# One root per block in the norms, and three constants loaded at other times, in a hybrid decoder layer on one core

## The chip, the cores and the metric
The kernel runs on one core of a Trainium2 chip. The metric is the device time of one execution in microseconds (us). The core has five instruction queues that run side by side and wait for each other by semaphores: TensorE (PE, matmuls and transposes), VectorE (DVE), ScalarE (ACT), GpSimd (POOL) and SyncE (SP, which here only issues DMAs; SPq in the trace). P is 128, the number of partitions; D is 1024, the width of the model.

## The reference
One layer over 1024 tokens and 16 meta tokens in front of them, all in float32. Two RMS norms stand in it: one with the scale vector g_mix ahead of the mixer (latent attention and retention, gated and merged), one with g_ffn ahead of the expert mixer (PEER).

```python
def rmsnorm(x, g):
    y = x * lax.rsqrt(jnp.mean(x * x, axis=-1, keepdims=True) + EPS)
    return y * g

def mixer_sublayer(h, pos, g_mix, w_in, ...):
    hn = rmsnorm(h, g_mix)
    z = hn @ w_in                          # queries, keys, values, gates of both branches
    ...
    merged = sigmoid(za) * y_a + sigmoid(zr) * y_r
    return merged @ w_mix_out

def peer_sublayer(h, g_ffn, w_peer_q, ...):
    x = rmsnorm(h, g_ffn)
    q = x @ w_peer_q                       # then top 16 of 128x128 experts per head, gathered and summed
    ...

h = h + mixer_sublayer(...);  h = h[:, N_META:];  h = h + peer_sublayer(...)
```

## The kernel before
The 1024 tokens are eight blocks of 128. They go in three groups, of three, two and three blocks; the first group carries the meta tokens as a fourth tile. Each group runs through the same stages, and a group's first stage is interleaved with the last part of the group before it.

- **latents (L345 to L372).** The blocks' x tiles are loaded (tile xt, L357; the meta rows L355), then g_mix, broadcast over the partitions (L360). `norm_scale` (L253) gives one scale per row, L363 multiplies xt by it and by g_mix, and PE transposes the result in 128x128 pieces (L272), four to a PSUM tile "tr" of which there are two. ACT copies the tile to hn_hi, the high part in fp32r (L275), and DVE takes the rest as hn_lo (L276); only then is the PSUM tile free again. In group 0 each block is transposed right behind its scale, in the others all at the end.
- **mix and merge.** The branches, their gates and the merge, whose result is mT (L857, L858). Queries go out to DRAM and back (qT_d, L557).
- **output (L868 on).** x is loaded again into h2 (L884), w_mix is multiplied and added into it block by block (`residual`, L886). Then g_ffn is loaded (L904), `norm_scale` runs over the h2 blocks, L908 makes xnt (two buffers), xnt is transposed into xT_hi and xT_lo, and the w_pq matmuls use those. The pool of g_ffn and xnt opens where that of mT has been closed, so the space of g_ffn is that of tiles that the last w_mix matmuls still read.
- Behind the groups stands the dense part of the experts (from about 1425 us to the end); rows gathered by POOL and dotted by DVE (L1071, L1088) run beside groups 1 and 2 and beside the dense part.

`norm_scale` squares a row and sums it on ACT (`square_sum`, L251), makes v = mean + eps on DVE (L262) and takes v to the power -0.5 on POOL (`rsqrt`, L213). It does so for block 0 alone, and then for all other blocks together, with one v and one root as wide as their number.

A dense product is three fp32r matmuls (`mm3`, L245 to L247): whi with hn_hi, with hn_lo, and wlo with hn_hi. Weights come through three "raw" buffers (L234) and are split by ACT (whi, L217) and DVE (wlo, L218).

At the top level the x tiles, the meta rows and g_mix of group 0 are issued first (`next(first)` runs up to the first yield of latents), then the constants (ident, g_cols, masks, iota, the rotary scales, keys), then HEAD = 20 further steps of group 0's latents, and then everything else. Routing (top experts per head) has its own pool, fc, opened at the head of output(); its tile "oh" (128x2048 in bf16, the same bytes as 128x1024 in float32) is used only while experts are picked.

A framework puts each engine's instructions into a static order and adds the waits. SP issues its DMAs strictly in that order, and one that waits holds those behind it.

Of the kernel before, what the change touches and what calls it, by code (L numbers as in the profile page):

```python
# [12 lines left out]
F32 = mybir.dt.float32  # L13
BF16 = mybir.dt.bfloat16
# [4 lines left out]
OP = mybir.AluOpType  # L19
# [4 lines left out]
P = 128  # L24
D = 1024
# [9 lines left out]
EPS = 1e-6  # L35
H = 8
# [11 lines left out]
DELAY = 8.0  # L48
STEPS = (((86, 72), (116, 64), (116, 144)), ((112, 90), (112, 100), (112,)), (80, 50))
HEAD = 20  # L50
BUBBLE = 12
LEAVE = ((6, 6, 3), (0, 1, 1))
RATES = ((0.0, 0.0), (0.5, 0.2), (0.3, 0.3), (0.8, 0.2), (0.9, 0.45), (0.0, 0.52))
# [91 lines left out]
def hybrid_layer(ctx: ExitStack, tc: tile.TileContext, out, a, dbg=None):  # L145
    nc = tc.nc
    V, S, T, G = nc.vector, nc.scalar, nc.tensor, nc.gpsimd
    dbg = dbg or {}

    const = ctx.enter_context(tc.tile_pool(name="const", bufs=1))  # L150
    work = ctx.enter_context(tc.tile_pool(name="work", bufs=2))
# [42 lines left out]
    def bcast(ap, n, off=0):  # L194
        return bass.AP(tensor=ap.tensor, offset=ap.offset + off, ap=[[0, P], [1, n]])
# [15 lines left out]
    def rsqrt(v, n, name, bufs=2):  # L211
        y = work.tile([P, n], F32, name=name, bufs=bufs)
        G.tensor_tensor(y, v, mhalf[:, 0:n], OP.pow)  # L213
        return y
# [34 lines left out]
    def square_sum(src, acc):  # L249
        junk = mw.tile([P, TW], F32, name="zt").bitcast(BF16)  # L250
        S.activation(junk[:, :src.shape[-1]], src, AF.Square, accum_out=acc)  # L251

    def norm_scale(tiles, name):  # L253

        n = len(tiles)
        ss = work.tile([P, n], F32, name=f"ss_{name}")
        v = work.tile([P, n], F32, name=f"v_{name}")
        for k in (slice(0, 1), slice(1, n)):
            for i in range(n)[k]:
                square_sum(tiles[i], ss[:, i:i + 1])  # L260
            if range(n)[k]:
                V.tensor_scalar(v[:, k], ss[:, k], 1.0 / D, EPS, op0=OP.mult, op1=OP.add)  # L262
                r = rsqrt(v[:, k], len(range(n)[k]), f"r_{name}{k.start}")
                for i in range(n)[k]:
                    yield i, r[:, i - k.start:i - k.start + 1]

    def transposed(dst, src, i):

# [46 lines left out]
    def group(g):  # L315
# [4 lines left out]
        meta, last = g == 0, g == len(GROUPS) - 1  # L320
# [4 lines left out]
        def pool(name, side="left"):  # L325
            return open_pool(f"{name}{g}", side)
# [20 lines left out]
        def latents():  # L347
            hn = own.hn
            nps, npool = pool("np")
            xs = []  # L350
            for b in every:
# [4 lines left out]
                else:  # L356
                    nc.sync.dma_start(xt, a["x"][P * b:P * b + P])  # L357
                xs.append(xt)
            g_mix = npool.tile([P, D], F32, name="g_mix")
            nc.sync.dma_start(g_mix, bcast(a["g_mix"], D))  # L360
            yield
            for i, r in norm_scale(xs, "x"):
                V.scalar_tensor_tensor(xs[i], xs[i], r, g_mix, op0=OP.mult, op1=OP.mult)  # L363
                yield
                if not g:
                    transposed(hn, xs[i], i)
            if g:
                for _ in range(BUBBLE):
                    yield
# [481 lines left out]
        def output():  # L851
# [4 lines left out]
            for c in range(KD):  # L856
                S.activation(mT[0][:, c], own.mg[:, c], AF.Copy, scale=0.5)  # L857
                V.scalar_tensor_tensor(mT[1][:, c], own.mg[:, c], 0.5, mT[0][:, c].bitcast(F32),  # L858
                                       op0=OP.mult, op1=OP.subtract)
# [12 lines left out]
            if not last:  # L872
                if g >= NGROUP:
                    ktp = ctx.enter_context(tc.tile_pool(name=f"kt{g}", bufs=1, side="right", reuse_waits="tile"))
                fcs, fc = pool("fc", "right")
# [4 lines left out]
            xT = [xp.tile([P, KD, W], F32R, name=n) for n in ("xT_hi", "xT_lo")]  # L880
            hps, hp_ = pool("h2", "right")
            h2 = hp_.tile([P, nbk, D], F32, name="h2")
            for i, b in enumerate(blocks):
                nc.sync.dma_start(h2[:, i], a["x"][P * b:P * b + P])  # L884
            def residual(i, c, z):
# [14 lines left out]


            fps, fp = pool("fp", "right")
            g_ffn = fp.tile([P, D], F32, name="g_ffn")
            nc.sync.dma_start(g_ffn, bcast(a["g_ffn"], D))  # L904
            for i, r in norm_scale([h2[:, i] for i in range(nbk)], "f"):
                b = blocks[i]
                xn = fp.tile([P, D], F32, name="xnt", bufs=2)
                V.scalar_tensor_tensor(xn, h2[:, i], r, g_ffn, op0=OP.mult, op1=OP.mult)  # L908
                nc.sync.dma_start(h2_d[b], h2[:, i])
                if g < NGROUP:  # L910
                    nc.sync.dma_start(xn_d[b], xn)
                transposed(xT, xn, i)
# [35 lines left out]

        own.right = g % 2 == 1
        own.open_inputs, own.latents, own.open_mix, own.mix = open_inputs, latents, open_mix, mix  # L950
        own.open_merge, own.merge, own.output = open_merge, merge, output
        return own
# [326 lines left out]
    first = groups[0].latents()  # L1279
# [5 lines left out]
    g_gn, g_ql, g_kvl = g_cols[:, 0:8], g_cols[:, 8:11], g_cols[:, 11:13]  # L1285
    g_gnh = const.tile([P, 8], F32, name="g_gnh")
    V.tensor_scalar(g_gnh, g_gn, 0.5, None, op0=OP.mult)
    mask_a, mask_r = (mw.tile([P, P], F32, name=n, bufs=1) for n in ("mask_a", "mask_r"))
    nc.sync.dma_start(mask_a, a["c_mask_a"])
    mask_b, ident_b = (mw.tile([P, P], BF16, name=n, bufs=1) for n in ("mask_b", "ident_b"))  # L1290
# [12 lines left out]
                                                      ap=[[1, 64], [1, 1]]))  # L1303
    gk96 = const.tile([P, 1], F32, name="gk96")
    V.tensor_tensor(gk96, gqk[:, 0:1], gqk[:, 1:2], OP.mult)
    ones = const.tile([P, 1], F32, name="ones")
    V.memset(ones, 1.0)
    keys = const.tile([P, 256], F32, name="keys")
    V.memset(keys, 0.0)
    nc.sync.dma_start(keys[0:64, 0:128], a["keys"][0:64])  # L1310
    nc.sync.dma_start(keys[64:128, 128:256], a["keys"][64:128])

    for _ in range(HEAD):
        next(first)
    interleave([first, groups[0].retentions], STEPS[2], 0)
    for n, now in enumerate(groups):
# [28 lines left out]
```

## Time and profile before

| | |
|---|---|
| median of 3 runs | 3475.97 us (3467.64 to 3477.73) |
| the profiled execution | 3464.74 us, of it 3463.0 us span |
| PE busy | 3293.4 us, 95% |
| PE weight loads (overlap PE) | 3003.2 us, 87% |
| DVE busy | 2609.1 us, 75% |
| ACT busy | 1266.3 us, 37% |
| POOL busy | 1118.6 us, 32% |
| DMA | 835.80 MB, 241 GB/s over the span |

The span is the time from the first to the last instruction of one profiled execution; all times of the trace are counted from its start. A row of the timeline reads: start, duration, engine, line, operation, what is written and what is read, shapes, count, and in brackets the idle time of the engine just before and what ended it. A row of the chain of waits is start, duration and piece of work.

### The profile page before, as it was taken

The page shows a single profiled execution, that of the slowest core. Times are in us where ns is not written, and L with a number is a line of the kernel's source. Part 1 is how long each engine was busy: PE and PEld are TensorE (multiplying, and loading weights), DVE is VectorE, ACT ScalarE, POOL GpSimd, SP SyncE. Part 2 cuts the span into 40 slices and gives each one's busy share as a digit, 9 for nine tenths or more (in the row PEclk, how much of TensorE's full clock was granted, in tenths as well). Part 3 has the DMA queues.
Part 4 walks back from the last instruction along what each step waited for, and adds up shares of the span by engine and source line. Part 5 has one row for each costly group of instructions (what it writes and reads, how often), then busy time and mean ns, then how long its engine had stood idle before and what let it go on. Part 6 is the DMA issues. An engine that isn't in the chain of part 4 may idle for free.

```text
span 3463.0 us, 53189 instructions
## 1 busy us (share of the span) xinstructions
PE 3293.4 (95%) x20376; PEld 3003.2 (87%) x20376; DVE 2609.1 (75%) x5118; ACT 1266.3 (37%) x2117; POOL 1118.6 (32%) x821
## 2 busy tenths in 40 slices
PE   8899999989889999999999999999999999999999
PEld 7788988888777799999999987988898888888888
DVE  4434458987697566689999786888788878878885
ACT  3445344554445533324666322222222222222221
POOL 0100010113211122012322444555556545555562
PEclk9999999999899999999999999999999999999999
DMA  4322354457744458545878998999889898989895
GB/s 133 124 72 92 122 178 149 142 178 242 261 149 149 132 199 293 174 158 197 312 287 297 350 313 288 338 316 325 312 308 342 297 327 311 337 309 326 303 327 188
DMA packets 326673, 835.80 MB, mean 241 GB/s; under 512 B 45697, under 2 KB 138113, under 8 KB 323601
## 3 DMA queue, kind: packets, MB, share of 16 engines
q1 hardware_dynamic: 215824, 429.69, 36.0%
q0 software_dynamic: 110592, 402.70, 33.0%
q8 instruction: 160, 2.62, 0.3%
q14 instruction: 97, 0.79, 0.1%
HBM read 753.85 MB, written 78.43 MB: 240 GB/s over the span
## 4 chain that ended last, share of the span: by engine, by line
PE 35%; issue 23%; POOL 10%; DVE 9%; DMA 7%; ACT 2%; SPq 0%; POOLq 0%; DVEq 0%; ACTq 0%
POOL row L1071 10%; PE zacc L245 7%; PE zacc L246 6%; PE zacc L247 6%; PE tr L245 3%; PE tr L246 3%; PE tr L247 3%; DMA row<-in_peer_v_dram,eidx 3%; DVE wlo L218 2%; DMA gl<-gl_d 2%; PE tr L766 2%; PE sc L730 1%; DVE row L1088 1%; DMA row<-in_peer_u_dram,eidx 1%; PE sc L776 1%
## 5 line engine op out<-in xcount | busy, mean ns | idle before, releaser
L217 ACT ACTIVATE whi<-raw 128x1024 fp32r<-128x1024 f32 (+2 forms) x508 | 520.4, 1026 | 1333.5 <-PE zacc L247 610.0
L218 DVE TENSOR_TENSOR wlo<-raw,whi 128x1024 fp32r<-128x1024 f32 (+2 forms) x508 | 599.7, 1181 | 405.6 <-ACT whi L217 404.9
L1071 POOL DMA_INDIRECT row<-in_peer_u_dram,eidx x384 | 500.0, 1302 | 992.7 <-DVE row L1088 761.2
L1071 POOL DMA_INDIRECT row<-in_peer_v_dram,eidx x384 | 555.2, 1446 | 649.7 <-DVE acc L1097 279.6
L245 PE MATMUL zacc<-whi,c_hi 128*128 128x512 f32 x1280 | 505.0, 395 | 36.8 <-DVE y L1270 34.4
L247 PE MATMUL zacc<-whi,c_lo 128*128 128x512 f32 x1280 | 503.1, 393 | 5.3 <-DVE c_lo L218 5.3
L246 PE MATMUL zacc<-wlo,c_hi 128*128 128x512 f32 x1280 | 502.6, 393 | 0.0
L1088 DVE SCALAR_TENSOR_TENSOR row<-row,xn 128x1024 f32<-128x1024 f32 x384 | 462.0, 1220 | 32.3 <-DMA row<-in_peer_u_dram,eidx 24.1
L245 PE MATMUL tr<-xT_hi,whi 128*128 128x384 f32 (+1 forms) x1216 | 411.7, 339 | 4.9 <-ACT gl L1181 3.8
L247 PE MATMUL tr<-xT_hi,wlo 128*128 128x384 f32 (+1 forms) x1216 | 408.9, 336 | 0.0
L246 PE MATMUL tr<-xT_lo,whi 128*128 128x384 f32 (+1 forms) x1216 | 408.8, 336 | 0.0
L245 PEld LDWEIGHTS zacc<-whi,c_hi 128*128 128x128 f32 x1280 | 243.4, 190 | 92.0 <-issue 32.1
L245 PE MATMUL tr<-x_hi,whi 128*128 128x256 f32 x1024 | 293.7, 287 | 0.6 <-DVE xT_lo L276 0.6
L247 PEld LDWEIGHTS zacc<-whi,c_lo 128*128 128x128 f32 x1280 | 243.0, 190 | 58.8 <-DVE c_lo L218 7.4
L246 PE MATMUL tr<-x_lo,whi 128*128 128x256 f32 x1024 | 289.1, 282 | 0.0
L247 PE MATMUL tr<-x_hi,wlo 128*128 128x256 f32 x1024 | 288.7, 282 | 0.0
L246 PEld LDWEIGHTS zacc<-wlo,c_hi 128*128 128x128 f32 x1280 | 243.6, 190 | 49.9
L1097 DVE SCALAR_TENSOR_TENSOR acc<-row,dots,acc 128x1024 f32<-128x1024 f32 x192 | 245.7, 1280 | 16.0 <-DMA row<-in_peer_v_dram,eidx 15.8
L245 PE MATMUL zacc<-whi,hn_hi 128*128 128x256 f32 x832 | 251.3, 302 | 6.4 <-DVE vr L680 4.1
L1097 DVE SCALAR_TENSOR_TENSOR xn<-row,dots,xn 128x1024 f32<-128x1024 f32 x189 | 241.7, 1279 | 11.8 <-DMA row<-in_peer_v_dram,eidx 11.7
L246 PE MATMUL zacc<-wlo,hn_hi 128*128 128x256 f32 x832 | 239.5, 288 | 0.9 <-DVE wlo L218 0.9
L245 PEld LDWEIGHTS tr<-xT_hi,whi 128*128 128x128 f32 x1216 | 232.0, 191 | 6.7 <-ACT gl L1181 4.4
(269 smaller groups left out, 6933.9 us busy)
## 6 DMA issues: line engine op xcount, KB each, us to landing
raw<-in_peer_ut_dram SPq DMA_DIRECT2D x128, 512.0 KB, 5.1
raw<-in_peer_vt_dram SPq DMA_DIRECT2D x128, 512.0 KB, 6.5
gate_d<-stage SPq DMA_DIRECT2D x20, 2048.0 KB, 7.8
gt<-gate_d SPq DMA_DIRECT2D x31, 1280.0 KB, 10.6
raw<-in_w_nat_dram SPq DMA_DIRECT2D x72, 512.0 KB, 3.5
raw<-in_w_z_dram SPq DMA_DIRECT2D x48, 512.0 KB, 3.4
gl_d<-gl SPq DMA_DIRECT2D x48, 320.0 KB, 3.3
gl<-gl_d SPq DMA_DIRECT2D x48, 320.0 KB, 8.1
```

Of the source, the lines that this page charges most:

```text
L217: S.activation(hi, src, AF.Copy)
L218: V.tensor_tensor(lo, src, hi.bitcast(F32), OP.subtract)
L245: T.matmul(o, st[0], mv[0], start=first, stop=False)
L246: T.matmul(o, st[0], mv[1], start=False, stop=False)
L247: T.matmul(o, st[1], mv[0], start=False, stop=last)
L730: T.matmul(sc[:, c, 0:w], qh, kT[0:96, k0:k0 + w], start=True, stop=c < nch - 1)
L766: T.matmul(oo, vh[:, c + k], pT[:, k], start=False, stop=c + k == b)
L776: T.transpose(pt[:, P * k:P * k + P], pr[:, k0:k0 + P], ident)
L1071: G.indirect_dma_start(out=row, out_offset=None, in_=table, in_offset=bass.IndirectOffsetOnAxis(ap=eidx[:, k:k + 1], axis=0))
L1088: op = V.scalar_tensor_tensor(row, row, 1.0, xn, op0=OP.mult, op1=OP.mult, accum_out=dots[:, k:k + 1])
L1097: op = V.scalar_tensor_tensor(acc[k % 2], row, dots[:, k:k + 1], acc[k % 2], op0=OP.mult, op1=OP.add)
```

## The change
`norm_scale` takes a v and a root for every block by itself. g_mix is loaded behind the first x tile and ahead of the others. In groups 0 and 1 g_ffn goes into the routing pool's tile "oh", viewed as 128x1024 float32, and its load stands ahead of the h2 loads; the last group keeps its own tile. At the top level, eight of the 20 steps of group 0's latents come ahead of the masks, iota, the rotary scales and the keys, and `ones` is set earlier.

```diff
+EARLY = 8
     def norm_scale(tiles, name):
-        n = len(tiles)
-        ss = work.tile([P, n], F32, name=f"ss_{name}")
-        v = work.tile([P, n], F32, name=f"v_{name}")
-        for k in (slice(0, 1), slice(1, n)):
-            for i in range(n)[k]:
-                square_sum(tiles[i], ss[:, i:i + 1])
-            if range(n)[k]:
-                V.tensor_scalar(v[:, k], ss[:, k], 1.0 / D, EPS, op0=OP.mult, op1=OP.add)
-                r = rsqrt(v[:, k], len(range(n)[k]), f"r_{name}{k.start}")
-                for i in range(n)[k]:
-                    yield i, r[:, i - k.start:i - k.start + 1]
+        for i, t in enumerate(tiles):
+            ss = work.tile([P, 1], F32, name=f"ss_{name}")
+            square_sum(t, ss)
+            v = work.tile([P, 1], F32, name=f"v_{name}")
+            V.tensor_scalar(v, ss, 1.0 / D, EPS, op0=OP.mult, op1=OP.add)
+            yield i, rsqrt(v, 1, f"r_{name}")
...
                 xs.append(xt)
-            g_mix = npool.tile([P, D], F32, name="g_mix")
-            nc.sync.dma_start(g_mix, bcast(a["g_mix"], D))
+                if len(xs) == 1:
+                    g_mix = npool.tile([P, D], F32, name="g_mix")
+                    nc.sync.dma_start(g_mix, bcast(a["g_mix"], D))
...
             h2 = hp_.tile([P, nbk, D], F32, name="h2")
+            if not last:
+                g_ffn = fc.tile([P, 8, 16, 2 * H], BF16, name="oh").rearrange("p a b c -> p (a b c)").bitcast(F32)
+                nc.sync.dma_start(g_ffn, bcast(a["g_ffn"], D))
             for i, b in enumerate(blocks):
                 nc.sync.dma_start(h2[:, i], a["x"][P * b:P * b + P])
...
             fps, fp = pool("fp", "right")
-            g_ffn = fp.tile([P, D], F32, name="g_ffn")
-            nc.sync.dma_start(g_ffn, bcast(a["g_ffn"], D))
+            if last:
+                g_ffn = fp.tile([P, D], F32, name="g_ffn")
+                nc.sync.dma_start(g_ffn, bcast(a["g_ffn"], D))
...
     V.tensor_scalar(g_gnh, g_gn, 0.5, None, op0=OP.mult)
+    ones = const.tile([P, 1], F32, name="ones")
+    V.memset(ones, 1.0)
+    for _ in range(EARLY):
+        next(first)
     mask_a, mask_r = (mw.tile([P, P], F32, name=n, bufs=1) for n in ("mask_a", "mask_r"))
...
-    for _ in range(HEAD):
+    for _ in range(HEAD - EARLY):
         next(first)
```

The lines of the changed kernel are shifted by a few: v is L260 there, the scale L360, hn_lo and xT_lo L272, wlo L219, xnt L909.

DVE at the start of the program, first before, then after; v_x is the mean of squares, xt the scaled tile, hn_lo what frees a transpose buffer.

```order
L262 TENSOR_SCALAR v_x<-ss_x 128x1
L262 TENSOR_SCALAR v_x<-ss_x 128x3
L363 SCALAR_TENSOR_TENSOR xt<-xt,r_x_163,g_mix 128x1024
L1287 TENSOR_SCALAR g_gnh<-g_cols 128x8
L1292 CAST ident_b<-ident 128x128
L363 SCALAR_TENSOR_TENSOR xt<-xt,r_x_187,g_mix 128x1024
L1291 CAST mask_b<-mask_a 128x128
L1296 CAST iota_i<-iota 128x256
L363 SCALAR_TENSOR_TENSOR xt<-xt,r_x_187,g_mix 128x1024
L276 TENSOR_TENSOR hn_lo<-tr,hn_hi 128x4x128
L1305 TENSOR_TENSOR gk_150<-gqk 128x1
L276 TENSOR_TENSOR hn_lo<-tr,hn_hi 128x4x128
```

```order
L260 TENSOR_SCALAR v_x<-ss_x 128x1
L360 SCALAR_TENSOR_TENSOR xt<-xt,r_x,g_mix 128x1024
L260 TENSOR_SCALAR v_x<-ss_x 128x1
L360 SCALAR_TENSOR_TENSOR xt<-xt,r_x,g_mix 128x1024
L260 TENSOR_SCALAR v_x<-ss_x 128x1
L360 SCALAR_TENSOR_TENSOR xt<-xt,r_x,g_mix 128x1024
L1288 TENSOR_SCALAR g_gnh<-g_cols 128x8
L260 TENSOR_SCALAR v_x<-ss_x 128x1
L1297 CAST ident_b<-ident 128x128
L360 SCALAR_TENSOR_TENSOR xt<-xt,r_x,g_mix 128x1024
L272 TENSOR_TENSOR hn_lo<-tr,hn_hi 128x4x128
L219 TENSOR_TENSOR wlo<-raw,whi 128x1024
```

Each scale now has its own v ahead of it, all four scales stand ahead of the first hn_lo (before, three), and a wlo follows that hn_lo; before, a second hn_lo, the scale of tile 3 and two more hn_lo came ahead of the first wlo.

DVE at the end of group 0's output stage, from its third-last residual add on, before and after; v_f is the mean of squares of an h2 block, xT_lo the counterpart of hn_lo.

```order
L886 TENSOR_TENSOR h_4889<-zacc,h_4889 128x256
L262 TENSOR_SCALAR v_f<-ss_f 128x1
L886 TENSOR_TENSOR h_4889<-zacc,h_4889 128x256 x2
L218 TENSOR_TENSOR wlo<-raw,whi 128x1024 x2
L262 TENSOR_SCALAR v_f<-ss_f 128x2
L908 SCALAR_TENSOR_TENSOR xnt<-h_4889,r_f_5257,g_ffn 128x1024
L908 SCALAR_TENSOR_TENSOR xnt<-h_4889,r_f_5282,g_ffn 128x1024
L276 TENSOR_TENSOR xT_lo<-tr,xT_hi 128x4x128 x2
L908 SCALAR_TENSOR_TENSOR xnt<-h_4889,r_f_5282,g_ffn 128x1024
L276 TENSOR_TENSOR xT_lo<-tr,xT_hi 128x4x128 x4
```

```order
L260 TENSOR_SCALAR v_f<-ss_f 128x1
L886 TENSOR_TENSOR h_4903<-zacc,h_4903 128x256
L260 TENSOR_SCALAR v_f<-ss_f 128x1
L886 TENSOR_TENSOR h_4903<-zacc,h_4903 128x256
L909 SCALAR_TENSOR_TENSOR xnt<-h_4903,r_f,oh 128x1024 x2
L260 TENSOR_SCALAR v_f<-ss_f 128x1
L219 TENSOR_TENSOR wlo<-raw,whi 128x1024
L272 TENSOR_TENSOR xT_lo<-tr,xT_hi 128x4x128 x2
L219 TENSOR_TENSOR wlo<-raw,whi 128x1024
L272 TENSOR_TENSOR xT_lo<-tr,xT_hi 128x4x128 x2
L909 SCALAR_TENSOR_TENSOR xnt<-h_4903,r_f,oh 128x1024
L272 TENSOR_TENSOR xT_lo<-tr,xT_hi 128x4x128 x2
```

The two wlo moved from ahead of the first xnt to places between the xT_lo, and xnt reads "oh".

SP around the same loads in group 0, before and after; acc is a first copy of h_d, the stored h2.

```order
L884 DMA h_4889<-in_x_dram 128x1024 x3
L234 DMA raw<-in_w_mix_dram 128x1024 x4
L234 DMA raw<-in_w_pq_dram 128x1024 x4
L909 DMA h_d<-h_4889 128x1024 x2
L1080 DMA acc<-h_d 128x1024
L904 DMA g_ffn<-in_g_ffn_dram 128x1024
L909 DMA h_d<-h_4889 128x1024
```

```order
L884 DMA h_4903<-in_x_dram 128x1024 x2
L882 DMA oh<-in_g_ffn_dram 128x1024
L884 DMA h_4903<-in_x_dram 128x1024
L235 DMA raw<-in_w_mix_dram 128x1024 x4
L235 DMA raw<-in_w_pq_dram 128x1024 x4
L910 DMA h_d<-h_4903 128x1024 x2
```

g_ffn's load went from behind the w_pq loads and two stores of h2 to a place among the h2 loads. In group 1 it went likewise from behind all w_mix loads to a place ahead of three of their issues, right behind a store of qT_d.

At the start SP issues, before: three x tiles, meta, g_mix, ident, g_cols, the masks, iota, the rotary scales, keys, two w_lat pieces, w_pe; after: x, g_mix, two x, meta, ident, g_cols, one w_lat piece, the masks, iota, the rotary scales, keys, w_lat, w_pe. PE's order is the same but for eight transposes that stand six matmuls earlier in group 2's latents.

## Rows read from the trace of the kernel before
**Rows 1.** The page, busy time: us, share of the span, instructions.

```profile
PE 3293.4 (95%) x20376; PEld 3003.2 (87%) x20376; DVE 2609.1 (75%) x5118; ACT 1266.3 (37%) x2117; POOL 1118.6 (32%) x821
```

**Rows 2.** Waits of PE, whole span: us in total, times, longest us.

```profile
PE tr L272 <- DVE xnt L908: 17.0, 3, 8.2
PE tr L272 <- DVE xt L363: 13.8, 2, 11.7
```

**Rows 3.** Timeline of all engines at the start of the kernel.

```profile
3.97 1.06 ACT L251 ACTIVATE zt<-xt 128x1024 bf16<-128x1024 f32 x1 [1.96 <-DMA xt<-in_x_dram]
...
5.15 0.15 DVE L262 TENSOR_SCALAR v_x<-ss_x 128x1 f32<-128x1 f32 x1 [2.06 <-ACT zt L251]
5.37 1.06 ACT L251 ACTIVATE zt<-xt 128x1024 bf16<-128x1024 f32 x1 [0.25 <-DMA xt<-in_x_dram]
5.39 0.57 POOL L213 TENSOR_TENSOR r_x<-v_x,mhalf 128x1 f32<-128x1 f32 x1 [4.96 <-DVE v_x L262]
...
8.02 1.06 ACT L251 ACTIVATE zt<-xt 128x1024 bf16<-128x1024 f32 x1 [1.50 <-DMA xt<-in_x_dram]
...
10.36 1.28 DVE L363 SCALAR_TENSOR_TENSOR xt<-xt,r_x,g_mix 128x1024 f32<-128x1024 f32 x1
10.49 1.88 POOL L213 TENSOR_TENSOR r_x<-v_x,mhalf 128x3 f32<-128x3 f32 x1 [4.52 <-DVE v_x L262]
...
11.70 1.97 PE L272 MATMUL tr<-ident,xt 128*128 128x128 f32 x8 [11.70 <-DVE xt L363]
...
12.40 1.29 DVE L363 SCALAR_TENSOR_TENSOR xt<-xt,r_x,g_mix 128x1024 f32<-128x1024 f32 x1 [0.54 <-POOL r_x L213]
...
15.13 0.68 DVE L276 TENSOR_TENSOR hn_lo<-tr,hn_hi 128x512 fp32r<-128x512 f32 x1
...
17.65 0.69 DVE L276 TENSOR_TENSOR hn_lo<-tr,hn_hi 128x512 fp32r<-128x512 f32 x1
...
19.45 1.22 DVE L218 TENSOR_TENSOR wlo<-raw,whi 128x1024 fp32r<-128x1024 f32 x1 [0.25 <-ACT whi L217]
...
23.00 1.28 DVE L276 TENSOR_TENSOR hn_lo<-tr,hn_hi 128x512 fp32r<-128x512 f32 x2
...
23.74 0.50 PE L246 MATMUL zacc<-hn_lo,whi 128*128 128x512 f32 x1 [0.34 <-DVE hn_lo L276]
```

**Rows 4.** Tile r_f, POOL: duration ns min/median/max, first and last start us, forms.

```profile
L213 POOL TENSOR_TENSOR r_f<-v_f,mhalf x6: 555/567/701, 513.3 to 1407.8; 128x1 f32<-128x1 f32 x4, 128x2 f32<-128x2 f32 x2
```

**Rows 5.** Chain of waits, group 0's output: start us, us, what.

```profile
517.35 6.60 DMA g_ffn<-in_g_ffn_dram
...
530.62 1.13 PE tr L272 x4
...
533.15 0.69 PE tr L245
...
538.64 0.32 PE tr L246
538.95 0.18 PE tr L247
```

**Rows 6.** Timeline of DVE, group 0's output.

```profile
517.36 0.42 DVE L886 TENSOR_TENSOR h<-zacc,h 128x256 f32<-128x256 f32 x1 [1.85 <-PE zacc L247]
...
524.05 2.48 DVE L908 SCALAR_TENSOR_TENSOR xnt<-h,r_f,g_ffn 128x1024 f32<-128x1024 f32 x2 [3.92 <-DMA g_ffn<-in_g_ffn_dram]
```

**Rows 7.** Waits of PE, 735 to 775 us, group 2's latents.

```profile
PE tr L272 <- DVE xt L363: 2.1, 1, 2.1
```

**Rows 8.** Windows: us, busy PE, PEld, DVE, ACT, POOL (x), PEclk, DMA share, GB/s.

```profile
758.00:760.00 2.00, 0.63 (x3) 0.34 (x3) 2.00 (x5) 1.46 (x3) 0.00 (x0) 0.50 0.56 227
...
913.69:922.46 8.77, 7.88 (x63) 7.48 (x63) 6.01 (x10) 2.12 (x2) 1.88 (x1) 1.00 1.01 391
```

**Rows 9.** Chain of waits, end of group 1's mix and output.

```profile
892.13 8.35 DMA qT_d<-headT
...
913.69 8.77 DMA raw<-in_w_pq_dram
```

More of the change, by code (lines that the diff above doesn't have):

```diff
@@ L1305, in hybrid_layer @@
     V.tensor_tensor(gk96, gqk[:, 0:1], gqk[:, 1:2], OP.mult)
-    ones = const.tile([P, 1], F32, name="ones")
-    V.memset(ones, 1.0)
     keys = const.tile([P, 256], F32, name="keys")
```

## The prediction
> **What bounds the kernel now.** I read the page first: TensorE (PE) is busy 95% of the span [rows 1]. So time is won only where PE waits, and what is won early is kept: from about 1425 us to the end every engine's queue holds the same instructions in the same order in both kernels. Next I read PE's waits over the whole span, summed by what they waited for. The two normalisations that the change touches stand there with 17.0 us in 3 waits (the output norm, tile xnt) and 13.8 us in 2 waits (the input norm, tile xt) [rows 2], 30.8 us or 0.9% together. That is all the change can take away directly. Then I read each place in the timeline and in the chain of waits: the start of the kernel, and the end of each group's output stage.
>
> **Part 1, the start.** The change puts g_mix second in SP's queue, takes one root per block, and moves constants back. Before, block 0 has its value v at 5.15 and its root (0.57) at 5.39, but its scale runs only at 10.36, since v of the other three stands ahead of it on DVE and g_mix comes fifth; the 128x3 root takes 1.88 from 10.49 [rows 3]. PE's first transpose waits for that scale, until 11.70 [rows 3]. The words of the change promise most here, so I worked it through.
> x1 now lands in the third slot of the queue; I give it x2's time, so that its square starts at 8.02 [rows 3]. From v to the end of the root 5.15 to 5.96 [rows 3], a hop of 0.04 to the scale as at the three-wide root (12.37 to 12.40) [rows 3]: 0.85 from v to scale. The square takes 1.18 to v (3.97 to 5.15) [rows 3]. So scale 1 starts at 8.02 + 1.18 + 0.85 = 10.05. On DVE v of the next block stands behind each scale, so the chain is serial from here: scale 1 to 11.33 (1.28 long), scale 2 from 12.18 to 13.46, scale 3 from 14.31 to 15.59. The last scale is done sooner than before. But the order of DVE puts the first hn_lo, which frees the PSUM buffer of the first transposes, behind scale 3 now: 15.6, against 15.13 before, when it stood ahead of that scale [rows 3].
> From there the two transpose buffers set the pace: one buffer goes from an hn_lo to the next in 2.52 (15.13 to 17.65) [rows 3]. A wlo of 1.22 [rows 3] now stands between the first and the second hn_lo, so the second buffer starts at 15.6 + 0.65 (an hn_lo) + 1.2 = 17.45, its next turns are 19.97 and 22.49, then comes another wlo, and tile 3's hn_lo is at 24.35. The first complete dense step (L246) follows it by 0.74 (23.00 to 23.74) [rows 3], at 25.1. Against 23.74 this is **+1.4**, a loss. Bounds: if x1 and x2 each land a slot sooner than I gave them (8.02 back to 5.37, the gap of two squares [rows 3]), the chain moves by -2.65 and the start is -1.25; if a single root on POOL costs what the three-wide one did, three times 1.31 more is +5.3. I take the 0.57, since every one-wide root of the trace is at it: four of the six r_f roots, minimum 0.555 and median 0.567, and the two-wide ones only 0.70 [rows 4].
> [...]
> The masks, iota and keys that are loaded later have users on DVE that now stand between hn_lo instructions; these are short casts, inside the wait for the buffer. The first w_lat load, moved ahead of them, feeds a wlo that DVE reaches only at 16.2. I cost both at nothing; the hn_lo cycle above hides them.
>
> **Part 2, group 0's output.** Here the gain is. In the chain of waits g_ffn's load starts at 517.35, behind the last w_mix matmul, and takes 6.60 to land [rows 5]; DVE's xnt idles 3.92 for it and runs at 524.05 [rows 6]. After the change the vector sits in a routing tile (free since the kernel began in this group), is loaded between the second and third h2 load about 480 us, and is long there. xnt of block 0 then waits for its buffer and stands behind the last residual add, at 517.36 for 0.42 [rows 6]: it starts at 517.7, block 1's at 519.0 (its v and root follow its own square now, and needn't wait for block 2's). Then v of block 2 and a wlo to 521.5, the two xT_lo of block 0 (0.65 each, like hn_lo) to 522.75, a wlo to 523.95, the two xT_lo of block 1 to 525.3, and only then xnt of block 2, to 526.6. Before, that last xnt ended at 529.97 and the transposes began at 530.62 [rows 5]; the first w_pq matmul came 2.53 later, at 533.15 [rows 5]. So now 526.6 + 2.53 = 529.1: **-4.0**. It isn't the whole 8.2 us of PE's wait, because the two wlo that ran inside that wait now stand between the steps of the norm.
> The clock is the open cost. The first dense matmuls after the wait run 0.32 us apart, at half the clock, until 538.95, where they become 0.18 [rows 5]. If the clock did not fall, (538.95 - 533.15) x (1 - 0.175/0.32) = 2.6 us would come on top. [...]
> [...]
> The load moved costs SP nothing that I can see: the w_mix loads behind it leave a transfer of 0.52 MB later, and none of PE's long waits there is for a load.
>
> **Part 3, groups 1 and 2.** Group 1's norm was already one root each, and its xnt is not among the waits for g_ffn. What changes is that its 0.52 MB no longer stand ahead of the w_pq loads, which take 8.77 to land in the chain of waits [rows 9]. At the 391 GB/s of that stretch [rows 8] they are 1.3 us; the residual add that PE waits for next hangs on PE's own last matmuls too, so I take **-0.7**, half of it, between 0 and -1.3. The load now goes out about 892, right behind a store of qT_d that itself is 8.35 in the chain [rows 9]; what that could cost is the slower rival. Group 1's input norm has the same order as before: 0. In group 2's, the first scale runs sooner and PE's 2.1 us wait [rows 7] can go, but the first hn_lo there still stands behind the third scale: 0, between -2.1 and the same size above. In group 2's output a root of 0.57 takes the place of one of 0.70 [rows 4]: **-0.1**. The five added v (0.15 each [rows 3]) and five added roots lie on engines that are not the bound.
>
> **Sum.** +1.4 - 4.0 - 0.7 - 0.1 = -3.4 us. The profiled execution took 3464.74 (span 3463.0 and 1.74 around it), so its like would be 3461.3. That execution is 11 us under the median of the runs, 3475.97, and the runs go from 3467.64 to 3477.73; the forecast goes by the median: 3475.97 - 3.4 = 3472.6. About 0.3% (10.4 us) is what a measurement of this kernel can tell from no change, so this is a gain that would read as "same".
>
> **Rivals.**
> 1. Clear gain. The clock stays up in group 0 (-2.6), x1 and x2 land a slot sooner at the start (-2.65), and group 2's wait of 2.1 goes: -3.4 - 7.35 = -10.75, 3465.2. For: each is a real row. Against: the clock row of group 2 [rows 8], and that all three must hold.
> 2. The vector isn't early. If the copy waits (SP holds it until the routing tile and a transfer slot are free) or xnt is late for another reason, the -4.0 is gone: +0.6, 3476.6. For: PE waits for xnt in all three groups [rows 2], and in the other two not for the vector. Against: in group 0 nothing has used the routing tile yet, and the idle time before xnt names g_ffn alone [rows 6].
> 3. Slower. Group 1's g_ffn collides with the qT_d store issued just ahead of it at 892.13. ACT's next headT copy waits for that store, and mT, w_mix and the end of the stage hang on it [rows 9]. If the store only shares with 0.52 MB, it lands 1.3 later; if it falls behind all of it, up to 8.35 more. It decides from 3.4 on: then the whole is slower. At its worst -3.4 + 8.35 = +4.95, 3480.9. For: that store is slow already, with loads beside it. Against: it is issued first.
>
> **How the numbers follow.** The forecast has 0.64; clear gain 0.15; the vector not early 0.08; slower 0.10 (with the +5.3 of the start in it too, past +0.3% only in 0.04); 0.03 for what I don't see. Faster by over 0.3%: the clear gain and a little of the forecast's own spread, 0.17. Slower by over 0.3%: 0.05. Within: 0.78. The range goes from the clear gain less 3 us for the scatter of the runs, 3462, to the slower rival and 1 us, 3482.
>
> **What would show it.** In the profile after: at the start, the first L272 transposes before 11.70, a serial row of v, root and scale on DVE and POOL, and the first L246 at 25 (wrong if it is under 22.5). In group 0's output, no idle time of xnt for g_ffn, xnt of block 0 at the last residual add + 0.4, and the stretch from there to the first w_pq matmul 11.7 long instead of 15.8; the clock down to 0.50 again or not tells forecast from clear gain. In group 1, headT's wait for qT_d at 5.8 or more. I'd be wrong if the span changes by more than 10 us with these rows as forecast: then it is the dense stages behind 1425 us, which I hold to be unchanged, that moved.

## The result

| | median | lowest to highest | runs |
|---|---|---|---|
| before | 3470.83 us | 3465.66 to 3480.21 | 11 |
| changed | 3488.51 us | 3480.86 to 3493.53 | 11 |

The changed kernel takes 1.0051 of the time before, 95% interval 1.0039 to 1.0063: 17.7 us slower, where the forecast was 3.4 us faster and the range ended at 3482. So the sign is wrong.

The page of the changed kernel (busy us, share of the span, instructions) has the same 20376 matmuls as before, but PE is busy 22 us longer than in [rows 1]:

```profile
span 3485.6 us, 53207 instructions
...
PE 3315.5 (95%) x20376; PEld 3023.0 (87%) x20376; DVE 2610.6 (75%) x5123; ACT 1265.7 (36%) x2117; POOL 1113.7 (32%) x826
```

PE's waits over the whole span (us in total, times, longest) are what the change worked on. Those for xnt went from 17.0 [rows 2] to 13.2, and the first wait of the kernel is now for ident instead of xt and 1.4 shorter:

```profile
PE tr L268 <- DVE xnt L909: 13.2, 4, 4.9
...
PE tr L268 <- DMA ident<-in_c_ident_dram: 10.3, 1, 10.3
```

So these waits fell and PE's busy time grew. Since PE's order is all but the same in both, the n-th matmul of one trace can be set beside the n-th of the other. That shows where the time comes from:

```
n-th matmul    before, at us    changed: later by
     0             11.70             -1.40
   100             38.00             +3.28
  3000            484.35             +3.33
  3500            572.60             -0.40
  4500            725.67             +2.82
  4900            785.04             +5.51
  6500           1043.82             +2.09
  9000           1438.83             +2.16
 10000           1600.05             +1.96
 15000           2420.54            +12.32
 20000           3382.97            +22.09
```

Up to 1600 us the change gains and loses single microseconds. That is within what single traces differ by: l256, both128 and r480, three runs below that keep the order of before and lose no time, stand 2.6, 7.4 and 2.4 us ahead of before at the 9000th matmul. At the 20000th they are within 3 us of it. So the 20 us that come behind 1600 us, steadily, are a real loss, in the dense part that the change doesn't touch and where all queues are the same.

There one can look at single matmuls. A row names the operand that streams through PE first and the one that is held in it second: in `xT_hi,whi` the weights whi are held. In the timeline of PE (start, duration, line, what) this is a run of 24 matmuls with 384 columns, its first one and the one behind it, before:

```profile
2441.27 0.34 PE L245 MATMUL tr<-xT_hi,whi 128*128 128x384 f32 x1
...
2445.43 0.28 PE L245 MATMUL tr<-x_hi,whi 128*128 128x256 f32 x1
```

and such a run in the changed kernel:

```profile
1715.26 0.34 PE L246 MATMUL tr<-xT_hi,whi 128*128 128x384 f32 x1
...
1719.49 0.39 PE L1133 MATMUL zacc<-ob,oa 128*128 128x128 f32 x2
```

4.16 us against 4.23 for 24 of them: 173 ns apart before, 176 now. Over the whole dense part the mean distances are 173.6 and 176.7 ns (384 columns, 2516 of them), 118.4 and 121.1 (256 columns, x_lo with whi), 226.8 and 227.0 (512 columns), 118.0 and 118.0 (128 columns, oa with ob). So it is not the clock: the granted clock of the dense part (from 1425 us on) is 0.99 in both traces, and only two of the four kinds are slower, by 1 to 2%. With 3.1 ns on 2516 matmuls and some 1.6 on 2520 (the mean over all products of 256 columns) that is about 12 of the 20 us. The rest stays open. In this trace it lies in waits and slow matmuls between the products of 512 columns, but such stretches are as long in traces of kernels that lose no time (both128, n_only), so one trace can't say whose they are. PE's wait for y, the longest in its list, doesn't follow the loss either: 34.4 us before, 39.0 in the changed kernel, 29.1 in w_only, the slowest of all.

What differs for those matmuls is not an instruction but where their operands lie. The tiles of `norm_scale` are small, and the change needs two names fewer (r_x1 and r_f1). Each had two buffers of 32 bytes per partition, so everything that is allocated behind them on that side of SBUF, the memory that holds the tiles, moved down by 128 bytes: the weights' tiles raw, whi and wlo, the gathered rows, gl, c_hi. On the other side xT, x_hi and x_lo stayed where they were (the routing tile moved). In the built programs whi lies at 39424 before and at 39296 now, and xT_hi of the last group at 178144 in both.

### The profile page after: what moved, and what is told of

Read it like the earlier page. It is cut to its first block, busy times and chain, and to the rows that moved or that the text cites. A ratio compares the mean times of both kernels' runs of the same rounds, so it can differ in the third digit from the quotient of the medians.

```text
span 3485.6 us, 53207 instructions
## 1 busy us (share of the span) xinstructions
PE 3315.5 (95%) x20376; PEld 3023.0 (87%) x20376; DVE 2610.6 (75%) x5123; ACT 1265.7 (36%) x2117; POOL 1113.7 (32%) x826
## 4 chain that ended last, share of the span: by engine, by line
PE 37%; issue 22%; POOL 10%; DVE 10%; DMA 7%; ACT 2%; POOLq 0%; SPq 0%; DVEq 0%; ACTq 0%
POOL row L1072 9%; PE zacc L246 7%; PE zacc L247 7%; PE zacc L248 7%; PE tr L246 3%; PE tr L247 3%; PE tr L248 3%; DMA row<-in_peer_v_dram,eidx 2%; DVE wlo L219 2%; PE tr L763 2%; DMA gl<-gl_d 1%; PE sc L727 1%; DVE row L1089 1%; DMA row<-in_peer_u_dram,eidx 1%; PE sc L773 1%
## 5 line engine op out<-in xcount | busy, mean ns | idle before, releaser
L219 DVE TENSOR_TENSOR wlo<-raw,whi 128x1024 fp32r<-128x1024 f32 (+2 forms) x508 | 599.7, 1181 | 422.1 <-ACT whi L218 418.2
L1098 DVE SCALAR_TENSOR_TENSOR xn<-row,dots,xn 128x1024 f32<-128x1024 f32 x189 | 241.4, 1277 | 13.3 <-DMA row<-in_peer_v_dram,eidx 13.2
L248 PE MATMUL zacc<-whi,hn_lo 128*128 128x256 f32 x832 | 237.2, 285 | 0.0
```

Source lines behind the costliest of these rows:

```text
L219: V.tensor_tensor(lo, src, hi.bitcast(F32), OP.subtract)
L248: T.matmul(o, st[1], mv[0], start=False, stop=last)
L1098: op = V.scalar_tensor_tensor(acc[k % 2], row, dots[:, k:k + 1], acc[k % 2], op0=OP.mult, op1=OP.add)
```

## The experiments

Two theories were on the table. **Place**: the addresses slow the matmuls. **Order**: the dense part is reached with other queues in flight and never recovers. In each set of runs the kernel before was timed beside them (medians 3466.1, 3466.6 and 3467.6); the ratios are to these.

**a_pad.** The changed kernel with the root's tile widened from 4 to 64 bytes, which puts the left side's tiles back.

```diff
-            yield i, rsqrt(v, 1, f"r_{name}")
+            y = work.tile([P, 16], F32, name=f"r_{name}")[:, 0:1]
+            G.tensor_tensor(y, v, mhalf[:, 0:1], OP.pow)
+            yield i, y
```

> The changed kernel with its root tile widened, so that the tiles behind it lie at the addresses that they had before (128 bytes higher than in the changed kernel); no instruction is added or moved. Place theory (the addresses slow the dense score matmuls): the 384-column matmuls of the dense part go back from 176.7 to 173.6 ns apart, and the time from 3488.5 to about 3473, some 2 us over before. Order theory (the dense part is slower because it is reached with other queues in flight): spacing stays at 176.7 and the time at 3488.

Measured: 3467.15, ratio 1.0007 (0.9992 to 1.0022), spacing 173.6 ns. The run of 24 in its timeline is 4.17 us again:

```profile
1737.27 0.34 PE L246 MATMUL tr<-xT_hi,whi 128*128 128x384 f32 x1
...
1741.44 0.51 PE L1135 MATMUL zacc<-ob,oa 128*128 128x128 f32 x3
```

The whole loss is gone, with no instruction changed.

**b_shift.** The other direction: the kernel before, with one name for its two roots.

```diff
-                r = rsqrt(v[:, k], len(range(n)[k]), f"r_{name}{k.start}")
+                r = rsqrt(v[:, k], len(range(n)[k]), f"r_{name}")
```

> The kernel before with one name for its two roots, so that the same tiles lie 128 bytes lower, as in the changed kernel; the order of all instructions is that of before. Place theory: spacing of the 384-column matmuls up to 176.7 ns and the time up by 12 to 16, to about 3485. Order theory: no difference from before, 3471.

Measured: 3490.46, ratio 1.0070 (1.0055 to 1.0084), spacing 176.7 ns:

```profile
1717.64 0.34 PE L245 MATMUL tr<-xT_hi,whi 128*128 128x384 f32 x1
...
1721.88 0.39 PE L1132 MATMUL zacc<-ob,oa 128*128 128x128 f32 x2
```

24 in 4.24 us. The order of before, and no faster than the changed kernel. The order theory falls by these two.

**b_ffn** and **b_start** do one part of the change alone, at the addresses of before: the early g_ffn, and the start (g_mix second, eight steps first) with the old norm.

```diff
+            if not last:
+                g_ffn = fc.tile([P, 8, 16, 2 * H], BF16, name="oh").rearrange("p a b c -> p (a b c)").bitcast(F32)
+                nc.sync.dma_start(g_ffn, bcast(a["g_ffn"], D))
             for i, b in enumerate(blocks):
                 nc.sync.dma_start(h2[:, i], a["x"][P * b:P * b + P])
```

> The kernel before with only g_ffn's early load into the routing tile; addresses of the left tiles as before. Prediction's sum for this part: -4.0 in group 0 and -0.7 in group 1, so about 3466. Slower rival (the load collides with the qT_d store in group 1): +1.3 to +8.35 there, 3468 to 3475.

Measured: 3461.91, ratio 0.9990 (0.9976 to 1.0003). In its trace the matmuls from the 3000th to the 3500th (group 0's output) gain 5.6 us on before. The nine runs that leave g_ffn alone gain 0.2 to 2.2 there, so most of it is the edit's. From the 5700th to the 6500th (group 1's output) it gains 5.2, but those nine gain 0.1 to 6.7 there, and that shows nothing. The direction is as expected, but the interval reaches 1.

```diff
+    for _ in range(EARLY):
+        next(first)
     mask_a, mask_r = (mw.tile([P, P], F32, name=n, bufs=1) for n in ("mask_a", "mask_r"))
```

> The kernel before with only the start changed: g_mix second and eight steps ahead of the masks; norm as before (one root for block 0, one for the rest). Prediction's reason (the serial chain of one root per block and the wlo between the first hn_lo cost +1.4): without that chain the start is 0 to -3, 3468 to 3471. Rival (the loads' order itself costs, since x1 and x2 land later and PE begins its dense steps at half clock): +2 to +4, 3473 to 3475.

Measured: 3465.68, ratio 1.0002 (0.9989 to 1.0014). The half clock of the rival is an estimate from the pace: the first dense matmuls of the changed kernel are 0.43 us apart and the later ones 0.23, 1.9 to 1, and at a granted clock of 0.50 (before, 533 to 538 us) it is 0.32 to 0.175, 1.8 to 1. The windows view doesn't show it; it has 1.00 from 25 to 29 us. b_start's 100th matmul is 0.25 us later than before, its 1000th 1.7 earlier. In total this is inconclusive: b_ffn, whose start is that of before, is 2.3 late at the 100th, so single traces differ by as much there. But one row bears on the prediction's reason. The first complete dense step comes at 23.40 here (first row) and at 23.56 in best, which has this start too; in the nine kernels with the start and the norm of before it comes at 23.3 to 24.6. Only with the new norm as well is it later, at 25.33 in the changed kernel and 25.10 in a_pad (second row):

```profile
23.40 0.63 PE L247 MATMUL zacc<-hn_lo,whi 128*128 128x512 f32 x1
```

```profile
25.10 0.63 PE L247 MATMUL zacc<-hn_lo,whi 128*128 128x512 f32 x1
```

So the order of the loads alone costs nothing there. The serial chain does, as the prediction had it, and only in the new order: n_only, with the new norm and the old start, is at 23.45.

**both128, w_only, l256, r480** ask what about the place is bad. All have the order of before. both128 adds a tile of 128 bytes on the right side to b_shift, so xT and x_hi go down with the weights. w_only is b_shift with a tile of 128 bytes behind wlo, so only raw, whi and wlo are lower.

```diff
+    gpad = gat.tile([P, 32], F32, name="gpad")
+    V.memset(gpad[:, 0:1], 0.0)
```

> The kernel before in its own order, left tiles 128 bytes lower (as in b_shift) and the right ones, xT and x_hi among them, 128 bytes lower too. Distance theory (weight operand whi and moving operand xT must not stand at a bad distance): the distance is that of before, so 173.6 ns for the 384-column matmuls and 3467. Boundary theory (the weight operand must start on a 512-byte boundary): still 176.7 ns and 3485 to 3490.

Measured: 3470.57, ratio 1.0009 (0.9994 to 1.0023), spacing 173.6 ns:

```profile
1717.11 0.34 PE L247 MATMUL tr<-xT_hi,whi 128*128 128x384 f32 x1
...
1721.28 0.39 PE L1134 MATMUL zacc<-ob,oa 128*128 128x128 f32 x2
```

Same weights' addresses as in the slow kernels, and fast. So it is neither operand's address by itself, but the two together: their distance.

```diff
+    wpad = wp.tile([P, 32], F32, name="wpad", bufs=1)
+    V.memset(wpad[:, 0:1], 0.0)
```

> The kernel before in its own order; only raw, whi and wlo lie 128 bytes lower, all tiles behind them at their old addresses. If the split weights' address is the cause: 176.7 ns and 3485 to 3490. If it is one of the other left tiles (gathered rows, gl, c_hi): 173.6 ns and about 3467.

Measured: 3497.25, ratio 1.0073 (1.0048 to 1.0098). 384 columns: 176.7 ns. And a new one: the matmuls of 512 columns, where c_hi is held and whi streams, are 232.5 ns apart instead of 226.8. In b_shift c_hi had moved along with whi, here it stayed. A run of 240 of them in this kernel, first one and the one behind it:

```profile
2684.10 0.39 PE L245 MATMUL zacc<-whi,c_hi 128*128 128x512 f32 x1
...
2739.86 0.28 PE L245 MATMUL tr<-x_hi,whi 128*128 128x256 f32 x1
```

and before:

```profile
2662.28 0.39 PE L245 MATMUL zacc<-whi,c_hi 128*128 128x512 f32 x1
...
2716.68 0.28 PE L245 MATMUL tr<-x_hi,whi 128*128 128x256 f32 x1
```

55.76 us against 54.40. A second pair of operands changes its pace when, and only when, its distance is changed, which again speaks for the distance. It isn't always a loss, though: the 256-column matmuls of the output stages, where mT is held and whi streams, also went from distance 0 to 128 here, and their mean spacing fell, from 119.9 ns (in all other kernels measured) to 118.7. Nor does the time follow from the pace alone: 3840 matmuls at 5.7 ns would be 22 us more than in b_shift, and the medians are 7 apart. Where the others went, no run was made to show.

```diff
-    mhalf = const.tile([P, 16], F32, name="mhalf")
-    V.memset(mhalf, -0.5)
+    mhalf = const.tile([P, 80], F32, name="mhalf")
+    V.memset(mhalf[:, 0:16], -0.5)
```

> The kernel before in its own order, left tiles 256 bytes higher: whi off its 512-byte boundary by half of it. Boundary theory with 512 bytes: slow, 176 ns or more, 3480 to 3490. If 256 bytes are enough: 173.6 ns, 3467. Distance theory tells nothing by itself here.

Measured: 3467.68, ratio 1.0005 (0.9988 to 1.0022), spacing 173.6 ns. A shift by 256 bytes changes nothing, so as far as this shift shows the distance counts modulo 256 bytes, and no 512-byte boundary is needed.

r480 has a tile of 480 bytes instead of 128 at gpad, and the weights in place.

> The kernel before in its own order, left tiles in place and the right ones 480 bytes lower, so that xT and x_hi (480 bytes over a 512-byte boundary before) start on one. Boundary theory for the weight operand alone: 173.6 ns, 3467. If the moving operand's boundary counts as well: below 173.6 ns and some us faster. Distance theory: some other spacing, up or down.

Measured: 3468.64, ratio 1.0004 (0.9987 to 1.0020); 384 columns 173.7 ns, 256 columns 119.8 instead of 118.4. Nothing is won by the boundary, and at a distance of 0 the 256-column matmuls lose 1.4 ns.

**l64, l128.** As l256, with mhalf 16 and 32 columns wider.

> Before in its own order, left tiles 64 bytes higher: the distance from xT to whi, counted modulo 256 bytes, goes from 32 to 96. If only distances near 128 are bad, 173.6 ns and 3467; if every step off 0 to 32 costs, between 173.6 and 176.7 and up to 3478.

Measured: 3481.06, ratio 1.0039 (1.0021 to 1.0058), spacing 174.0 ns. This one stays open: half a nanosecond on some 2500 matmuls is 1 to 2 us, and the time rose by 13. In its profiled execution PE waits 43.0 us for y where it waited 34.4, and the granted clock of its runs is lower, 0.9785 at the median against 0.981 before. Why at this place, no run shows.

> Before in its own order, left tiles 128 bytes higher, the other way than in the changed kernel: distance 160 modulo 256, the same as there. Distance theory: 176.7 ns, 3485 to 3490. A theory by which lower addresses as such are slow: 173.6 ns and 3467.

Measured: 3491.06, ratio 1.0070 (1.0045 to 1.0094), spacing 176.7 ns. Up or down by 128 bytes is the same.

The distances, from the addresses in the built programs, in one table (bytes modulo 256; mean spacing in the dense part in ns):

```
           whi - xT   c_hi - whi   384 col.   512 col.   ratio to before
before         32          0         173.6      226.8       1
l256           32          0         173.6      226.8       1.0005
both128        32          0         173.6      226.8       1.0009
a_pad          32          0         173.6      226.8       1.0007
r480            0          0         173.7      227.0       1.0004
l64            96          0         174.0      227.0       1.0039
changed       160          0         176.7      227.0       1.0051
b_shift       160          0         176.7      227.0       1.0070
l128          160          0         176.7      227.0       1.0070
w_only        160        128         176.7      232.5       1.0073
```

**best, n_only.** With the place held, which parts are worth having? best has the new start and the early g_ffn with the old norm; n_only has only the new norm, as in a_pad.

> Before with the new start and the early g_ffn, but the old norm (one root for block 0, one for the rest); left tiles at their old addresses. Sum of the two parts as the traces of b_ffn and b_start showed them at 1425 us (-6.4 and about -1.7): -8, near 3459, ratio 0.9975 to 0.998. If the parts don't add, 3462 to 3466.

Measured: 3458.80, ratio 0.9974 (0.9961 to 0.9986): 9 us faster than before, and against the changed kernel's 1.0051 some 27 us. It beats both.

> Before with only the norm changed to one root per block, its root tile widened so that the addresses stay. If the serial chain costs, as a_pad against b_ffn and b_start suggests: +3 to +6 at 1425 us, about 3470. If one root per block costs nothing: 3466.

Measured: 3464.85, ratio 0.9994 (0.9979 to 1.0009): nothing by itself. Yet best and a_pad differ in the norm alone, their intervals don't overlap, and their ratios are 11 us apart. The rows explain some 3 of these. At the start the first complete dense step is at 25.10 in a_pad, at 23.56 in best and at 23.45 in n_only, so the norm costs 1.5 with the new start and nothing without it. In group 2's latents PE waits 2.4 for hn_lo in a_pad and 0.7 in best. Where the other 8 come from is not settled.

## Why the prediction was wrong

**The step that failed** is the one ahead of the sum: that "what is won early is kept", since from 1425 us on "every engine's queue holds the same instructions in the same order in both kernels". The queues are the same, and the pace is not. No part of the sum had a term for where tiles lie, no rival had it, and the last sentence of the prediction (the span moves by more than 10 us although the rows are as forecast: then the dense part moved) only named the symptom. That is what came: 20 us in the dense part, from 128 bytes; with the tiles put back (a_pad) all of it went.

**The sum by itself** comes out near zero, not at -3.4. As the rows below show them, its terms are +1.6 at the start, -4.0 in group 0 and +2.4 in group 2; group 1 shows nothing. That agrees with a_pad's 1.0007 at the addresses of before; its interval, 0.9992 to 1.0022, begins just above the forecast's 0.9990. (That a_pad's trace is 3.1 us ahead of before at the 9000th matmul, close to 3.4, says nothing, since traces of the same order scatter by more there.)

**Group 0's output, forecast -4.0.** In the changed kernel, timeline of DVE:

```profile
520.69 0.42 DVE L886 TENSOR_TENSOR h<-zacc,h 128x256 f32<-128x256 f32 x1 [0.48 <-PE zacc L248]
521.03 2.47 DVE L909 SCALAR_TENSOR_TENSOR xnt<-h,r_f,oh 128x1024 f32<-128x1024 f32 x2
...
528.60 1.27 DVE L909 SCALAR_TENSOR_TENSOR xnt<-h,r_f,oh 128x1024 f32<-128x1024 f32 x1
```

No idle time for g_ffn any more, where [rows 6] had 3.92; xnt follows the start of the last residual add by 0.34 (forecast 0.4). The chain of waits has the first w_pq matmul and the end of the slow ones:

```profile
532.51 0.69 PE tr L246
...
537.68 0.25 PE tr L246
```

From the last residual add to that matmul 11.82 (forecast 11.7; before 15.79): -3.97. The window of 524 to 526 us (busy time of PE, PEld, DVE, ACT, POOL, then PEclk, DMA share, GB/s) shows the clock at 0.51 although the wait is gone:

```profile
524.00:526.00 2.00, 0.64 (x3) 0.65 (x4) 2.00 (x4) 0.20 (x1) 1.11 (x1) 0.51 1.04 412
```

Before, it was 0.50 from 533 to 538 us, now it is 0.50 from 524 to 537. So the 2.6 us of the clear-gain rival did not come, as [rows 7, 8] spoke against it: in group 2 PE waits 2.1 us for xt, and the granted clock is 0.50 in 758 to 760. In the changed kernel PE's waits from 480 to 545 us are all for DVE (4.5 for xnt, 2.4 for xT_lo, 0.9 for nat), none for a DMA, and the clock fell all the same. PE's gaps there, one ahead of the window and one in it, are under 2 us each:

```profile
522.46 1.06 PE L268 MATMUL tr<-ident,xnt 128*128 128x128 f32 x8 [1.80 <-DVE xnt L909]
525.36 1.97 PE L268 MATMUL tr<-ident,xnt 128*128 128x128 f32 x8 [1.84 <-DVE xT_lo L272]
```

**The start, forecast +1.4.** Timeline of the changed kernel:

```profile
6.56 1.28 DVE L360 SCALAR_TENSOR_TENSOR xt<-xt,r_x,g_mix 128x1024 f32<-128x1024 f32 x1 [1.27 <-DMA g_mix<-in_g_mix_dram]
...
9.83 1.29 DVE L360 SCALAR_TENSOR_TENSOR xt<-xt,r_x,g_mix 128x1024 f32<-128x1024 f32 x1 [0.67 <-POOL r_x L214]
...
10.30 1.94 PE L268 MATMUL tr<-ident,xt 128*128 128x128 f32 x8 [10.30 <-DMA ident<-in_c_ident_dram]
...
13.47 0.55 POOL L214 TENSOR_TENSOR r_x<-v_x,mhalf 128x1 f32<-128x1 f32 x1 [1.60 <-DVE ident_b L1297]
...
15.26 0.68 DVE L272 TENSOR_TENSOR hn_lo<-tr,hn_hi 128x512 fp32r<-128x512 f32 x1
...
24.13 1.28 DVE L272 TENSOR_TENSOR hn_lo<-tr,hn_hi 128x512 fp32r<-128x512 f32 x2
...
25.33 0.63 PE L247 MATMUL zacc<-hn_lo,whi 128*128 128x512 f32 x1
25.75 0.63 PE L248 MATMUL zacc<-hn_hi,wlo 128*128 128x512 f32 x1
...
28.74 0.57 PE L246 MATMUL zacc<-hn_hi,whi 128*128 128x512 f32 x1
29.15 0.39 PE L247 MATMUL zacc<-hn_lo,whi 128*128 128x512 f32 x1
29.38 0.39 PE L248 MATMUL zacc<-hn_hi,wlo 128*128 128x512 f32 x1
```

The serial chain is as worked out: scale 1 at 9.83 (10.05), the first hn_lo at 15.26 (15.6), tile 3's at 24.13 (24.35), the first complete step at 25.33 (25.1). PE doesn't even use the early scale, since ident lands at 10.30. The root on POOL is 0.55. Against 23.74 this is +1.59, with +1.4 forecast. The dense matmuls now begin 0.43 us apart, and only from 29.15 on 0.23, as they were before:

```profile
24.32 0.39 PE L245 MATMUL zacc<-hn_hi,whi 128*128 128x512 f32 x1
...
24.55 0.40 PE L246 MATMUL zacc<-hn_lo,whi 128*128 128x512 f32 x1
```

That is some 2 us more (+3.28 at the 100th matmul in this trace, +1.85 in a_pad), but it isn't shown to be the change's: in b_ffn, with the start of before, they are 0.43 apart until 27.96.

One price is misleading, though it didn't enter the sum. By the 1.88 of the three-wide root [rows 3], three one-wide roots of 0.57 look cheaper than it. In best, with the same three-wide root and the same shapes, it takes 0.86:

```profile
12.05 0.86 POOL L214 TENSOR_TENSOR r_x<-v_x,mhalf 128x3 f32<-128x3 f32 x1 [5.92 <-DVE v_x L263]
12.94 1.28 DVE L365 SCALAR_TENSOR_TENSOR xt<-xt,r_x,g_mix 128x1024 f32<-128x1024 f32 x1 [0.98 <-POOL r_x L214]
```

What differs is DVE. Before, the root starts at 10.49 while DVE runs a scale from 10.36 to 11.64 [rows 3]; in best DVE does nothing beside it. In b_ffn, b_shift, both128, l256, r480, l64 and l128, which keep the old start and the old norm, it is 1.86 to 1.88 again, with the scale beside it, and in b_start 0.86 with none. So the root took 1.02 us longer where a scale ran beside it, which had 1.15 still to run. Why, the runs don't show. Three roots of 0.55, 1.65 together, are dearer than one of 0.86.

**Group 1, forecast -0.7.** The slower rival did not come: ACT's wait for the qT_d store was 5.8 us before (first row) and is 5.4 in the changed kernel.

```profile
ACT headT L482 <- DMA qT_d<-headT: 5.8, 1, 5.8
```

```profile
ACT headT L479 <- DMA qT_d<-headT: 5.4, 1, 5.4
```

Whether the -0.7 came can't be told. From the 5700th to the 6500th matmul the changed kernel gains 3.8 us and b_ffn 5.2, but both128, r480 and n_only, where this load is as before, gain 6.6, 6.7 and 5.6.

**Group 2's norm, forecast 0 with ±2.** PE's waits there rose by 2.4 us, a little past the range (from the 4500th to the 4900th matmul the loss is 2.7, in a_pad 2.5). Before, PE waited 2.1 for xt [rows 7] and 1.4 for hn_lo (first fence); now it waits 3.5 for a split weight and 2.4 for hn_lo (second fence). In best, with the old norm, it is 3.5 and 0.7 (third fence):

```profile
PE tr L272 <- DVE hn_lo L276: 1.4, 1, 1.4
```

```profile
PE zacc L246 <- ACT whi L218: 3.5, 1, 3.5
PE tr L268 <- DVE hn_lo L272: 2.4, 1, 2.4
```

```profile
PE zacc L246 <- ACT whi L218: 3.5, 1, 3.5
PE tr L273 <- DVE hn_lo L277: 0.7, 1, 0.7
```

So the wait for the weight isn't the norm's. It stands in the four kernels that load g_mix ahead of the other x tiles (2.7 in b_start) and is 0.3 at most in the rest. The prediction counted that order for group 0 alone, but every group has it. In group 2 the second x tile lands later, ACT stands 4.15 us for it, 2.08 for the last x tile before, and the split of the next weights follows behind the squares:

```profile
756.74 1.06 ACT L252 ACTIVATE zt<-xt 128x1024 bf16<-128x1024 f32 x1 [4.15 <-DMA xt<-in_x_dram]
...
761.08 1.08 ACT L218 ACTIVATE whi<-raw 128x1024 fp32r<-128x1024 f32 x1
```

The longer wait for hn_lo, 1.7 over best, is the norm's.

## What to carry to other kernels

Before a stage is called unchanged because its instructions are, compare the addresses of its operands as well: a change in the size or number of small tiles moves every tile behind them (here by 128 bytes). When a trace drifts steadily in a stage that nobody touched, compare the spacing of like matmuls there, kind by kind, and then test it with padding, which costs one run. Measure an edit with the layout held fixed, and keep from it the parts that pay: here the early vector and the new start together (0.26%), without the new norm. Which of these two pays is not shown, since each alone is inside the noise. And before one trace is set beside another, look at how far traces of the same order lie apart: here up to 7 us at one matmul.

## What the runs showed of the hardware

In these runs a matmul's pace changed with the distance in SBUF between the operand that is held and the one that streams. fp32r with 384 columns ran 173.7 ns apart at a distance of 0 bytes modulo 256, 173.6 at 32, 174.0 at 96 and 176.7 at 160 (+1.8%). With 256 columns (x_lo with whi) it was 118.4 at 32, 119.8 at 0 and 121.1 at 160. With 512 columns it was 226.8 to 227.0 at 0 and 232.5 at 128 (+2.5%). With 256 columns and mT held it was 119.9 at 0 and 118.7 at 128, so no one distance was best for all. In this kernel 128 bytes of padding were worth 0.5 to 0.7% of the time. Why, the runs don't show; nor whether other types or shapes behave like this.

A GpSimd root of 128x3 took 0.86 us with nothing on DVE beside it (best, b_start) and 1.86 to 1.88 beside DVE's scale of 1.28 (before and seven others).
